# First attention group normalised and rotated at the start instead of behind the gates; the sums of squares of every head taken in two spaced halves

## The chip, the core and the metric

The kernel runs on one core of a Trainium2 chip. The metric is the device time of one execution in microseconds (us). The core's engines work side by side, each through its own queue in order: TensorE (PE in the rows; PEld is its weight load), VectorE (DVE), ScalarE (ACT), GpSimd (POOL), and SyncE (SP), which here issues most of the transfers. POOL issues the rest.

## The reference

Two encoder layers over 512 tokens plus 16 learned meta tokens (T = 528 columns), width 2048, float32. The change lies in layer 0:

```python
def attention_mixer(h, w_in, q_norm, k_norm, w_out, ang_row, ang_col):
    proj = h @ w_in
    q, k, v, gate = jnp.split(proj, [...], axis=-1)      # 16 heads, 8 kv heads, width 128
    q = apply_axial_rope(rmsnorm(q, q_norm), ang_row, ang_col)
    k = apply_axial_rope(rmsnorm(k, k_norm), ang_row, ang_col)
...
    return (o * jax.nn.silu(gate)) @ w_out               # o: softmax attention
```

`h` is the RMS-normalised input. Each key/value head serves two query heads, so there are eight groups of one K, two Q and one V projection. Layer 1 (gated linear attention) is the same in both kernels.

## The kernel before

**Numbers.** Every product is made of three fast matmuls: operands are split in a high and a low part, and hi·hi, hi·lo, lo·hi are summed in PSUM. The normalised, transposed input lies in `uh`/`ul` for the whole layer. A weight block of 8 k-steps is loaded raw into `wraw` (two buffers), cast by ACT to `whi` and subtracted by DVE to `wlo` (three buffers each).

**Order.** A `Clock` decides the order in which the program is written: loops on PE call `clk.step`, generators driven by it (`combine`, `attention`) and calls put off with `clk.after(us, f)` are written in between when their time has come by that clock. `clk.flush` writes all that is still put off. A list scheduler then makes each engine's queue from it, with weights at a higher priority.

**Stages of layer 0.**

1. *Start, 0 to 57 us.* x is transposed and split while the first three column tiles of 128 are accumulated in six PSUM banks. In the kernel before these are gate tiles 0 to 2 (columns 4096 and on); they go to DRAM (`g_d`).
2. *Four projections, 57 to 106 us.* `to_dram` computes K, both Q and V of group 0 and stores them raw (`qkv_d`). Beside it `combine` builds `th`/`tl` on DVE and ACT in eight k-steps: sums of quarters of `uh`/`ul`. Its scratch tiles `x` are four quarter buffers, used in turn (step 2 and step 6 use the same one, `x02`).
3. *Five pairs of gate tiles, 106 to 208 us.* `seven` computes a pair with seven products of 24 matmuls instead of eight. A pair needs four raw quarter blocks, a11, a21, a22 and a12. For the first pair they are loaded into the two `wraw` buffers and into quarter buffers that `combine` has left: a22 in `x00`, a12 in `x02`. The order of products is a11·u, then T2, T3, T4, T1 (from `th`), then a12·u and one more.
4. *Group 0, about 208 to 310 us*, attention of group 0, with the projections for group 1 beside it. `first_group` first loads K and Q back, squares and scales them, and rotates three heads.
5. *Groups 1 to 7, 310 to 795 us*, each attention with the projections for the next group beside it, then output projection and layer 1.

**One head.** `take` makes `qw` (scaled) and `sq` (squares) from PSUM. `rope` swaps neighbouring blocks of 32 partitions with four transfers (`qs<-qw`, issued by SP), multiplies `qw` by cos and `qs` by sin on POOL, and some 6.5 us of the `Clock` later calls `late`: for each half of the columns two matmuls with ones sum the squares over partitions (`ssq`, L310 and L311) and a DVE instruction takes the sums out (L312); then rsqrt on ACT, `qw + qs` (L314), times the rsqrt, split. In the attention stages the `ssq` tile lies in `ps_o`, a pool of one bank which also holds the attention's output `o`, so the second half waits until DVE has read the first, and a following `o` until it has read the second.

Of the kernel before, what the change touches and what calls it, by code (L numbers as in the profile page):

```python
# [35 lines left out]
SLOTS = (3.1, 3.8, 3.8, 3.8, 3.8, 3.8, 3.8, 2.6)  # L36
# [46 lines left out]
def hybrid_encoder(  # L83
# [22 lines left out]
    qkv_d = scratch.tile([4, P, T], F32, name="qkv_d")  # L106
# [12 lines left out]
    rows = const.tile([P, P], F32, name="rows")  # L119
    rows0 = const.tile([KT, P], F32, name="rows0")  # L120
    G.memset(rows, 0.0)
    cols = const.tile([P, P], F32, name="cols")
    nc.sync.dma_start(out=rows0, in_=pre_norm[0].rearrange("(r p) -> r p", p=P))

# [87 lines left out]
    def seven(src, c, ys, th, tl, free):  # L212
# [53 lines left out]
        w = parts(a12)  # L266
        sums(a11, a12, a11)
        add(y1[:, l], product(w, of_u(1, 0)), y1[:, l])
# [26 lines left out]
    def rope(qw, sq, outs, ps_t, wait=6.5):  # L295
# [22 lines left out]
        clk.after(wait, late)  # L318

    def qk_tiles():  # L320
        kh = wk.tile([P, T], F32R, tag="kh", name="kh")
        kl = wk.tile([P, T], F32R, tag="kl", name="kl")

        qh = wk.tile([P, 2 * T], F32R, tag="qh", name="qh")
        ql = wk.tile([P, 2 * T], F32R, tag="ql", name="ql")
# [3 lines left out]
    Q1 = T + META  # L329

    st = ExitStack()
    sp = pool(st, "start")
    s2 = pool(st, "start2", 2)
    ps_g = pool(st, "ps_g", space=PSUM)
    ps_t = pool(st, "ps_t", 2, space=PSUM)
    xt = sp.tile([P, 4, D], F32, name="xt")
# [1091 lines left out]
```

## Time and profile before

| what | value |
|---|---|
| median of 3 runs | 1829.26 us (1827.41 to 1831.79) |
| the profiled execution, its own time | 1830.27 us |
| its span in the trace | 1828.5 us |
| what lies around the span | 1.8 us |
| PE busy | 1769.3 us, 97% of the span |
| mean granted clock of PE | 0.991 of full speed |

The span is what the rows below are cut from: a time of 106 us is 106 us behind the span's start. PE is the engine that is nearly always at work; a microsecond in which it waits, or in which its clock stands at half, is part of the time.

### The profile page before, as it was taken

How to read it: one execution, taken by the hardware profiler on the slowest of the kernel's cores; microseconds unless marked ns; L12 is line 12 of the kernel's file. 1: busy time of each engine (PE TensorE's matmuls, PEld its weight loads, DVE VectorE, ACT ScalarE, POOL GpSimd, SP SyncE). 2: the span in 40 equal slices, each digit the busy share in tenths (PEclk: the TensorE clock that was granted, in tenths of full speed). 3: DMA queues.
4: the chain of work that ended last, by engine and by line, in shares of the span. 5: the costliest groups of instructions: out<-in, count | busy, mean ns of one | idle time of the engine just before them, and what ended most of it. 6: DMA issues, size and time to landing. Idle time of an engine off the chain costs nothing. (4 is left out here: it accounts for less than half of the span.)

```text
span 1828.5 us, 31687 instructions
## 1 busy us (share of the span) xinstructions
PE 1769.3 (97%) x12591; PEld 1662.5 (91%) x12591; DVE 1121.6 (61%) x1904; ACT 950.8 (52%) x1909; POOL 219.7 (12%) x290
## 2 busy tenths in 40 slices
PE   8999899999989999999999999999999999999998
PEld 7999889998989999999999989998898988888886
DVE  4777586665656665752228697768585775764224
ACT  5543465555545554553237634458575775763221
POOL 3100222112121101021111101110010100000000
PEclk9999999999999999999999999999999999999999
DMA  8444433232322223253335344443332332344333
GB/s 254 140 139 118 145 91 97 71 93 77 89 76 81 72 84 99 68 173 93 92 105 169 119 133 128 125 119 97 86 110 77 104 100 77 103 156 165 100 93 127
DMA packets 266660, 203.11 MB, mean 111 GB/s; under 512 B 9900, under 2 KB 239984, under 8 KB 265984
## 3 DMA queue, kind: packets, MB, share of 16 engines
q1 hardware_dynamic: 254768, 162.79, 31.0%
q0 software_dynamic: 11744, 38.30, 6.0%
q8 instruction: 99, 1.62, 0.4%
q14 instruction: 49, 0.40, 0.1%
HBM read 165.47 MB, written 29.09 MB: 106 GB/s over the span
## 5 line engine op out<-in xcount | busy, mean ns | idle before, releaser
L158 PE MATMUL pp<-uh,whi 128*128 128x264 f32 (+1 forms) x2320 | 714.7, 308 | 1.7 <-DVE gr L617 1.6
L159 PE MATMUL pp<-ul,whi 128*128 128x264 f32 (+1 forms) x2320 | 705.1, 304 | 2.2 <-DVE ul L419 2.2
L160 PE MATMUL pp<-uh,wlo 128*128 128x264 f32 (+1 forms) x2320 | 705.8, 304 | 0.4 <-POOL wlo L358 0.3
L136 DVE TENSOR_TENSOR wlo<-wraw,whi 128x1024 fp32r<-128x1024 f32 (+1 forms) x239 | 291.1, 1219 | 312.2 <-ACT whi L135 311.4
L158 PEld LDWEIGHTS pp<-uh,whi 128*128 128x128 f32 x2320 | 440.0, 190 | 18.2 <-DVE gr L617 1.8
L160 PEld LDWEIGHTS pp<-uh,wlo 128*128 128x128 f32 x2320 | 439.9, 190 | 17.5 <-POOL wlo L358 0.6
L159 PEld LDWEIGHTS pp<-ul,whi 128*128 128x128 f32 x2320 | 440.3, 190 | 16.3 <-DVE ul L419 2.8
L135 ACT CAST whi<-wraw 128x1024 fp32r<-128x1024 f32 (+1 forms) x239 | 248.9, 1043 | 319.3 <-PE pp L159 127.7
L135 ACT CAST whi<-x 128x1024 fp32r<-128x1024 f32 x48 | 50.1, 1046 | 70.8 <-PE pp L236 50.1
L631 ACT ACTIVATE pn<-s,mx 128x528 f32<-128x528 f32 (+1 forms) x72 | 50.4, 700 | 57.1 <-DVE mx L628 56.5
L1340 PE MATMUL f<-whi,ul 128*128 128x512 f32 x192 | 75.6, 394 | 0.0
L1338 PE MATMUL f<-whi,uh 128*128 128x512 f32 x192 | 75.5, 393 | 0.0
L1339 PE MATMUL f<-wlo,uh 128*128 128x512 f32 x192 | 75.3, 392 | 0.0
L237 PE MATMUL pp<-uh,wlo 128*128 128x264 f32 x264 | 75.2, 285 | 0.0
L235 PE MATMUL pp<-uh,whi 128*128 128x264 f32 x264 | 75.0, 284 | 0.0
L236 PE MATMUL pp<-ul,whi 128*128 128x264 f32 x264 | 74.7, 283 | 0.0
L136 DVE TENSOR_TENSOR wlo<-x,whi 128x1024 fp32r<-128x1024 f32 x48 | 58.6, 1222 | 20.5 <-ACT whi L135 20.5
L304 POOL TENSOR_TENSOR qw<-qw,cos 128x528 f32<-128x528 f32 x24 | 32.1, 1339 | 293.2 <-DMA qs<-qw 293.2
L628 DVE TENSOR_REDUCE mx<-s 128x1 f32<-128x528 f32 (+1 forms) x72 | 50.7, 704 | 22.3 <-PE s L625 21.3
L645 ACT CAST ph<-pT 128x512 fp32r<-128x512 f32 (+1 forms) x80 | 40.7, 509 | 43.6 <-PE pT L641 34.9
L646 DVE TENSOR_TENSOR pl<-pT,ph 128x512 fp32r<-128x512 f32 (+1 forms) x80 | 47.4, 593 | 21.4 <-ACT ph L645 20.7
L235 PE MATMUL pp<-th,whi 128*128 128x264 f32 x192 | 56.1, 292 | 0.3 <-ACT th L135 0.3
(400 smaller groups left out, 3717.7 us busy)
## 6 DMA issues: line engine op xcount, KB each, us to landing
wraw<-in_attn_w_in_dram SPq DMA_DIRECT2D x82, 512.0 KB, 4.1
wraw<-in_gla_w_in_dram SPq DMA_DIRECT2D x81, 512.0 KB, 3.9
wraw<-in_attn_w_out_dram SPq DMA_DIRECT2D x32, 512.0 KB, 3.8
wraw<-in_gla_w_out_dram SPq DMA_DIRECT2D x32, 512.0 KB, 3.8
x<-in_gla_w_in_dram SPq DMA_DIRECT2D x15, 512.0 KB, 4.3
qs<-qw SPq DMA_DIRECT2D x96, 66.0 KB, 2.6
x<-in_attn_w_in_dram SPq DMA_DIRECT2D x12, 512.0 KB, 4.1
x<-h_d SPq DMA_DIRECT2D x32, 132.0 KB, 3.5
```

The source lines that it names most:

```text
L135: A.copy(hi, src)
L136: V.tensor_tensor(lo, src, hi.bitcast(F32), op=ALU.subtract)
L158: PE.matmul(ps, wh, uh[:, k, a:b], start=first, stop=False)
L159: PE.matmul(ps, wh, ul[:, k, a:b], start=False, stop=False)
L160: PE.matmul(ps, wl, uh[:, k, a:b], start=False, stop=last)
L235: PE.matmul(ps, w[0][:, k], bh[:, k], start=k == 0, stop=False)
L236: PE.matmul(ps, w[0][:, k], bl[:, k], start=False, stop=False)
L237: PE.matmul(ps, w[1][:, k], bh[:, k], start=False, stop=k == KH - 1)
L628: V.reduce_max(mx, s, axis=AX.XY, negate=True)
L1338: PE.matmul(ps, uh[:, k, ts], wh[:, kk], start=(k == 0), stop=False)
L1339: PE.matmul(ps, uh[:, k, ts], wl[:, kk], start=False, stop=False)
L1340: PE.matmul(ps, ul[:, k, ts], wh[:, kk], start=False, stop=(k == KT - 1))
```

## The change

The start accumulates K and both Q of group 0 (columns 2048, 0 and 128) in place of gates 0 to 2. They are evacuated with scale and square (two ACT instructions for each bank in place of one copy) and rotated there, one head after the other with a `clk.flush` after each, with `cos` and `sin` loaded into the start's own pool and the `ssq` tiles in the start's PSUM pool. The rotated tiles stay in a pool of the whole layer (`c0`) through the pairs. `to_dram` then computes gates 0 to 2 and V of group 0. `first_group` is gone, and the transfers of K and Q to DRAM and back with it.

The first pair is told `late=True`: its second product is a12·u, which needs no sums, and T2 comes third; a12·u is copied by ACT and added on DVE.

In `rope` the first half of the sum of squares is put off by 4.4 and the second half, with all that follows, by 6.5 (before: both by 6.5, or 4.5 in `first_group`). `SLOTS[0]`, the spacing of group 0's attention, goes from 3.1 to 3.8; the leads in front of groups 0 and 1 go; V of group 0 is put off by 8.0 in place of 5.0. Tiles of q and k alternate between two pools of one buffer.

```diff
-SLOTS = (3.1, 3.8, 3.8, 3.8, 3.8, 3.8, 3.8, 2.6)
+SLOTS = (3.8, 3.8, 3.8, 3.8, 3.8, 3.8, 3.8, 2.6)
...
-    def seven(src, c, ys, th, tl, free):
+    def seven(src, c, ys, th, tl, free, late=False):
...
         A.copy(y1[:, l], product(w, of_u(0, 0)))
+        if late:
+            w = parts(a12)
+            A.copy(y2[:, l], product(w, of_u(1, 0)))
         add(y1[:, r], product(parts(a11), of_t(T2)), y1[:, l])
+        if late:
+            add(y1[:, l], y1[:, l], y2[:, l])
...
-        w = parts(a12)
+        if not late:
+            w = parts(a12)
         sums(a11, a12, a11)
-        add(y1[:, l], product(w, of_u(1, 0)), y1[:, l])
+        if not late:
+            add(y1[:, l], product(w, of_u(1, 0)), y1[:, l])
...
-        qw = wk.tile([P, T], F32, tag="qw", name="qw", bufs=3)
-        sq = wk.tile([P, T], F32, tag="sq", name="sq", bufs=2)
+        qw = wk.tile([P, T], F32, tag="qw", name="qw", bufs=2)
+        sq = wk.tile([P, T], F32, tag="sq", name="sq", bufs=1 if wk is ws else 2)
...
+        def sums(a, b):
+            ps = ps_q.tile([P, 512], F32, tag=tag, name="ssq")[:, :b - a]
+            PE.matmul(ps, ones_r, sh[:, a:b], start=True, stop=False)
+            PE.matmul(ps, ones_r, sl[:, a:b], start=False, stop=True)
+            V.scalar_tensor_tensor(f[:, a:b], ps, 1.0 / P, erow[:, a:b], op0=ALU.mult, op1=ALU.add)
+
         def late():
-            for a, b in HALVES:
-                ps = ps_o.tile([P, 512], F32, tag="o", name="ssq")[:, :b - a]
-                PE.matmul(ps, ones_r, sh[:, a:b], start=True, stop=False)
-                PE.matmul(ps, ones_r, sl[:, a:b], start=False, stop=True)
-                V.scalar_tensor_tensor(f[:, a:b], ps, 1.0 / P, erow[:, a:b], op0=ALU.mult, op1=ALU.add)
+            sums(*HALVES[1])
             rsqrt_inplace(f)
...
-        clk.after(wait, late)
+        clk.after(4.4, lambda: sums(*HALVES[0]))
+        clk.after(6.5, late)
...
-    group([(w_in0, 4096, P), (w_in0, 4096 + P, 256)], accs, start, 0, halves=3,
+    group([(w_in0, 2048, P), (w_in0, 0, 256)], accs, start, 0, halves=3,
...
+    cos, sin = [ws.tile([P, T], F32, name=n, bufs=1) for n in ("cos0", "sin0")]
+    nc.sync.dma_start(out=cos, in_=rope_cos)
+    nc.sync.dma_start(out=sin, in_=rope_sin)
+    for i in range(3):
+        rope(*(taken(i) if i else head0), qks[0][1][i], ps_t, "t")
+        clk.flush()
     st.close()
...
-    for i, c in enumerate((2048, 0, P, 3072)):
-        to_dram(qkv_d, i, c)
+    for i, (dst, c) in enumerate([(g_d[i], 4096 + i * P) for i in range(3)] + [(v0_d, 3072)]):
+        to_dram(dst, i, c)
...
-        free = seven(w_in0, 4096 + h * P, ys, th, tl, free)
+        free = seven(w_in0, 4096 + h * P, ys, th, tl, free, h == 3)
...
-        lead = first_group(first_outs) if g == 0 else iter([7.0] if g == 1 else [])
-        att = clk.drive(chain(lead, att))
+        att = clk.drive(att)
```

**DVE behind the start.** In the kernel before, `combine` (L204, its first sum) follows right behind `erow`, the last piece of the row norms:

```order
L485 TENSOR_SCALAR erow<-rrow 128x528
L204 TENSOR_TENSOR x_751<-uh,ul 128x1056
L204 TENSOR_TENSOR x_752<-uh,ul 128x1056
L206 TENSOR_TENSOR x_751<-x_751 128x528
L206 TENSOR_TENSOR x_752<-x_752 128x528
```

In the changed kernel the three rotations stand between. These are the last twelve rows up to `combine` (L198 there); L313 takes a sum of squares, L318 is `qw + qs`, L319 the product with the rsqrt, `ql` the low part of a rotated head:

```order
L318 TENSOR_TENSOR qw<-qw,qs 128x528
L319 TENSOR_TENSOR qw<-qw,sq 128x528
L130 TENSOR_TENSOR ql_98<-qw,qh_97 128x528
L130 TENSOR_TENSOR sl<-sq,sh 128x528
L313 SCALAR_TENSOR_TENSOR sq<-ssq,erow 128x264 x2
L130 TENSOR_TENSOR wlo<-wraw,whi 128x1024
L318 TENSOR_TENSOR qw<-qw,qs 128x528
L319 TENSOR_TENSOR qw<-qw,sq 128x528
L130 TENSOR_TENSOR wlo<-wraw,whi 128x1024
L130 TENSOR_TENSOR ql_98<-qw,qh_97 128x512
L130 TENSOR_TENSOR ql_98<-qw,qh_97 128x16
L198 TENSOR_TENSOR x_843<-uh,ul 128x1056
```

What moved: the first instruction of `combine` stands behind the whole of the second and the third head. Six `wlo` stood inside `combine` up to the end of its step 6 in the kernel before; now four of them stand ahead of it, two inside, and two sums of the first pair (L224) inside too.

**SP, from the swaps to the first pair's blocks, in the changed kernel.** L301 is a swap, L147 a raw weight block of a projection, L211 a block of a pair (`x_843` is a22, `x_845` is a12; the bracket names the queues and engines that it waits for):

```order
L301 DMA qs<-qw 32x528 [waits DMAHW1_49,DMAHW2_49,DMAHW0_49,DMAHW7_49,DVE_49,Activation_49]
L301 DMA qs<-qw 32x528
L301 DMA qs<-qw 32x528 [waits DMAHW5_49]
L147 DMA wraw<-in_attn_w_in_dram 128x8x128 [waits DMAHW6_49,DVE_49]
L301 DMA qs<-qw 32x528
L147 DMA wraw<-in_attn_w_in_dram 128x8x128 [waits DVE_49]
L301 DMA qs<-qw 32x528 [waits DMAHW4_49,DMAHW5_49,DMAHW3_49,DMAHW7_49,DVE_49,Activation_49]
L301 DMA qs<-qw 32x528 x3
L147 DMA wraw<-in_attn_w_in_dram 128x8x128 [waits DMAHW6_49,DVE_49]
L211 DMA wraw<-in_attn_w_in_dram 128x8x128 [waits DMAHW0_49,DVE_49]
L211 DMA wraw<-in_attn_w_in_dram 128x8x128 [waits DMAHW5_49,DVE_49]
L211 DMA x_843<-in_attn_w_in_dram 128x8x128 [waits DMASW4_49,DMASW2_49,DMASW6_49,DMASW1_49,DMASW7_49,DMASW0_49,DVE_49]
```

The next row is `x_845`, the load of a12. What moved: the swaps of group 0 stood at the beginning of the attention; here a head's swaps wait for DVE's reading of the head before (one buffer `qs`), one of them stands behind a raw block, and a12, needed sixth before, is needed second.

**PE in the first pair of the changed kernel**, from the end of the first product over six matmuls of scores (`s`) to the second product, which is the first row with a wait:

```order
L232 MATMUL pp<-uh,wlo 128x264
L626 MATMUL s<-kh_95,qh_97 128x264
L627 MATMUL s<-kh_95,ql_98 128x264
L628 MATMUL s<-kl_96,qh_97 128x264
L626 MATMUL s<-kh_95,qh_97 128x264
L627 MATMUL s<-kh_95,ql_98 128x264
L628 MATMUL s<-kl_96,qh_97 128x264
L230 MATMUL pp<-uh,whi 128x264 [waits Activation_49]
L231 MATMUL pp<-ul,whi 128x264
L230 MATMUL pp<-t0h,whi 128x264 [waits Activation_49]
L231 MATMUL pp<-t0l,whi 128x264
L232 MATMUL pp<-uh,wlo 128x264 [waits DVE_49]
```

In the kernel before T2 (`t0h`) came second. Here two of its matmuls come third and fourth within a12·u.

**PE at the third head of a group** (the projections for group 3, beside group 2's attention). Before, eight rows stand between the halves (before the first row here), and five between the second half and the first `o`:

```order
L310 MATMUL ssq<-sh,ones_r 128x264 [waits DVE_49]
L311 MATMUL ssq<-sl,ones_r 128x264
L160 MATMUL pp<-uh,wlo 128x264
L158 MATMUL pp<-uh,whi 128x264
L159 MATMUL pp<-ul,whi 128x264
L160 MATMUL pp<-uh,wlo 128x264
L158 MATMUL pp<-uh,whi 128x264
L661 MATMUL o<-ph,vh 128x272 [waits DVE_49,Activation_49]
```

In the changed kernel 21 rows stand between the halves (before the first row here), and nine between the second half and `o`:

```order
L311 MATMUL ssq<-sh,ones_r 128x264 [waits DVE_49]
L312 MATMUL ssq<-sl,ones_r 128x264
L152 MATMUL pp<-uh,whi 128x264
L153 MATMUL pp<-ul,whi 128x264
L154 MATMUL pp<-uh,wlo 128x264
L152 MATMUL pp<-uh,whi 128x264
L153 MATMUL pp<-ul,whi 128x264
L154 MATMUL pp<-uh,wlo 128x264
L152 MATMUL pp<-uh,whi 128x264
L153 MATMUL pp<-ul,whi 128x264
L154 MATMUL pp<-uh,wlo 128x264
L664 MATMUL o<-ph,vh 128x272 [waits DVE_49,Activation_49]
```

What moved: the second half now waits for a DVE instruction that has had more time, and `o` still follows closely on it. On DVE at this head the order is now first half out, `gr` times `rrow` (L604, a stored gate), `qw + qs`, second half out; before it was `gr`, `qw + qs`, and then both halves out.

## Rows read from the trace of the kernel before

**Rows 1.** Windows: stretch, length, busy PE PEld DVE ACT POOL, PE's clock, DMA:

```profile
57.00:106.00 49.00, 49.00 (x406) 49.00 (x405) 45.17 (x65) 23.00 (x36) 3.50 (x7) 1.00 0.47 144
106.00:208.00 102.00, 102.00 (x841) 102.00 (x840) 74.96 (x87) 38.35 (x41) 9.03 (x18) 1.00 0.42 124
208.00:310.00 102.00, 89.75 (x690) 86.53 (x690) 69.49 (x129) 60.48 (x129) 27.80 (x25) 0.95 0.36 106
310.00:387.00 77.00, 73.32 (x587) 71.94 (x586) 50.47 (x105) 42.87 (x98) 12.70 (x12) 0.98 0.29 83
690.00:795.00 105.00, 100.28 (x811) 97.65 (x810) 70.40 (x142) 57.64 (x130) 10.84 (x10) 1.00 0.32 99
```

**Rows 2.** Waits of PE, 208 to 310 us: total, count, longest:

```profile
PE vps L552 <- DMA vt<-qkv_d: 4.5, 1, 4.5
PE ssq L311 <- DVE sl L136: 3.4, 2, 3.1
```

**Rows 3.** Waits of PE, 310 to 795 us, the longest sum:

```profile
PE ssq L310 <- DVE sq L312: 20.5, 12, 3.4
```

**Rows 4.** Timeline of PE at second halves: start, length, wait in brackets:

```profile
320.37 0.39 PE L310 MATMUL ssq<-sh,ones_r 128*128 128x264 f32 x1 [1.07 <-DVE sq L312]
...
357.93 0.39 PE L310 MATMUL ssq<-sh,ones_r 128*128 128x264 f32 x1 [1.92 <-DVE sq L312]
...
435.14 0.39 PE L310 MATMUL ssq<-sh,ones_r 128*128 128x264 f32 x1 [2.35 <-DVE sq L312]
...
658.60 0.39 PE L310 MATMUL ssq<-sh,ones_r 128*128 128x264 f32 x1 [1.74 <-DVE sq L312]
```

**Rows 5.** Timeline of DVE at the third head whose half PE awaits until 435.14:

```profile
433.13 0.87 DVE L601 TENSOR_TENSOR gr<-gr,rrow 128x528 f32<-128x528 f32 x1 [3.28 <-DMA gr<-g_d]
433.93 0.69 DVE L314 TENSOR_TENSOR qw<-qw,qs 128x528 f32<-128x528 f32 x1
434.66 0.43 DVE L312 SCALAR_TENSOR_TENSOR sq<-ssq,erow 128x264 f32<-128x264 f32 x1
435.69 0.43 DVE L312 SCALAR_TENSOR_TENSOR sq<-ssq,erow 128x264 f32<-128x264 f32 x1 [0.60 <-PE ssq L311]
```

**Rows 6.** Timeline of DVE, 57 to 106 us:

```profile
59.00 2.36 DVE L136 TENSOR_TENSOR wlo<-wraw,whi 128x1024 fp32r<-128x1024 f32 x2
...
62.49 2.42 DVE L204 TENSOR_TENSOR x<-uh,ul 128x1056 f32<-128x1056 f32 x2
...
97.31 1.26 DVE L136 TENSOR_TENSOR t0l<-x,t0h 128x1056 fp32r<-128x1056 f32 x1
```

**Rows 7.** Swaps and rotation: SP's queue in group 0, then the tile `qs`:

```profile
240.10 2.42 SPq L299 DMA_DIRECT2D qs<-qw  x4
...
L305 POOL TENSOR_TENSOR qs<-qs,sin x24: 1297/1316/1853, 223.7 to 725.0; 128x528 f32<-128x528 f32 x24
...
DMA to landing us min/median/max: 1.9/2.6/4.9
```

**Rows 8.** Groups of DVE instructions, 62.4 to 98.6 us: busy, mean ns, idle before:

```profile
L136 DVE TENSOR_TENSOR wlo<-wraw,whi 128x1024 fp32r<-128x1024 f32 x6 | 7.4, 1225 | 1.8 <-ACT whi L135 1.8
```

**Rows 9.** The page: cast of a quarter block (busy, mean ns), its transfer (us to landing):

```profile
L135 ACT CAST whi<-x 128x1024 fp32r<-128x1024 f32 x48 | 50.1, 1046 | 70.8 <-PE pp L236 50.1
...
x<-in_attn_w_in_dram SPq DMA_DIRECT2D x12, 512.0 KB, 4.1
```

**Rows 10.** Timeline of PE, first matmuls of the first pair's two first products:

```profile
106.11 0.28 PE L235 MATMUL pp<-uh,whi 128*128 128x264 f32 x1
...
109.01 0.29 PE L235 MATMUL pp<-t0h,whi 128*128 128x264 f32 x1
```

**Rows 11.** Windows of PE alone around its longest wait in group 0:

```profile
222.00:225.00 3.00, 3.00 (x15) 0.50 0.00 0
```

**Rows 12.** Timeline of DVE in group 0, the subtraction `sl` of two heads:

```profile
215.94 0.71 DVE L136 TENSOR_TENSOR sl<-sq,sh 128x528 fp32r<-128x528 f32 x1
...
236.50 1.80 DVE L136 TENSOR_TENSOR sl<-sq,sh 128x528 fp32r<-128x528 f32 x1
```

More of the change, by code (lines that the diff above doesn't have):

```diff
@@ L1 @@
 import heapq
-from itertools import chain
 from contextlib import ExitStack
@@ L293, in take, with rope @@
         return qw, sq, evac
-    def rope(qw, sq, outs, ps_t, wait=6.5):
+    def rope(qw, sq, outs, ps_q, tag):
         qs = wk.tile([P, T], F32, tag="qs", name="qs", bufs=1)
@@ L317, in late, with qk_tiles @@
                 split(hi, lo, qw[:, a:b])
-        clk.after(wait, late)
[L320 to L325, printed above, removed]
+        clk.after(4.4, lambda: sums(*HALVES[0]))
+        clk.after(6.5, late)
+    def qk_tiles(p, n):
+        kh, kl = [p.tile([P, T], F32R, name=f"k{w}{n}") for w in "hl"]
+        qh, ql = [p.tile([P, 2 * T], F32R, name=f"q{w}{n}") for w in "hl"]
         outs = ([(kh, kl, 0, T)], [(qh[:, :T], ql[:, :T], 0, T)],
@@ L335, in hybrid_encoder @@
     ps_t = pool(st, "ps_t", 2, space=PSUM)
+    rows = sp.tile([P, P], F32, name="rows")
+    rows0 = sp.tile([KT, P], F32, name="rows0")
+    G.memset(rows, 0.0)
+    nc.sync.dma_start(out=rows0, in_=pre_norm[0].rearrange("(r p) -> r p", p=P))
     xt = sp.tile([P, 4, D], F32, name="xt")
@@ L347, in load_w @@
     def load_w(i, k, m, queue=nc.sync):
-        raw, c, n = ((raw0, 4096, P), (raw1, 4096 + P, 256))[i]
+        raw, c, n = ((raw0, 2048, P), (raw1, 0, 256))[i]
         queue.dma_start(out=raw[:, k * n:(k + m) * n].rearrange("p (k n) -> p k n", n=n),
@@ L466, in hybrid_encoder, with taken @@
     V.tensor_scalar(col(QN), col(QN), SCALE, None, op0=ALU.mult)
-    for i in range(3):
-        y = s2.tile([P, T], F32, tag="y", name="y", bufs=3)
+    def taken(i):
+        qw, sq, evac = take(col(QN if i else KN))
         for j, ps, a, b in banks:
             if j == i:
-                A.copy(y[:, a:b], ps)
-        nc.gpsimd.dma_start(out=g_d[i], in_=y)
+                evac(ps, a, b)
+        return qw, sq
+    head0 = taken(0)
     V.reduce_sum(ss, ssq, axis=AX.X)
@@ L492, in hybrid_encoder @@
     th, tl = [ta.tile([P, KH, 4 * HALF], F32R, name=f"t0{w}") for w in "hl"]
+    quarters = [ta.tile([P, 4 * HALF], F32, name=f"x0{i}") for i in range(4)]
     yp = pool(la, "yp0", 2)
-    quarters = [ta.tile([P, 4 * HALF], F32, name=f"x0{i}") for i in range(4)]
     def y_tiles():
@@ L544, in values @@
         if g == 0:
-            nc.sync.dma_start(out=vt, in_=qkv_d[3])
+            with tc.high_priority(AHEAD):
+                nc.sync.dma_start(out=vt, in_=v0_d)
         else:
@@ L564, in late @@
                                    op0=ALU.mult, op1=ALU.subtract)
-        clk.after(1.2 if g else 5.0, late)
+        clk.after(1.2 if g else 8.0, late)
         return vh, vl, vm
     def qkv(g):
-        qk, outs = qk_tiles()
-        vv = values(g) if g == 1 else None
+        qk, outs = qks[g % 2]
         for i, c in enumerate((2048 + g * P, 2 * g * P, (2 * g + 1) * P)):
@@ L573, in qkv @@
             project(w_in0, c, HALVES, evac)
-            rope(qw, sq, outs[i], ps_t)
-        return qk, vv or values(g)
-    def first_group(outs):
-        qws = []
-        for i in range(3):
-            qws.append(wk.tile([P, T], F32, tag="qw", name="qw", bufs=3))
-            nc.gpsimd.dma_start(out=qws[i], in_=qkv_d[i])
-        for i in range(3):
-            yield 4.6 if i else 1.0
-            one_head(qws[i], outs[i], i)
-        yield 5.0
-    def one_head(qw, outs, i):
-        sq = wk.tile([P, T], F32, tag="sq", name="sq", bufs=2)
-        A.activation(sq, qw, AF.Square)
-        A.activation(qw, qw, AF.Copy, scale=col(QN if i else KN))
-        rope(qw, sq, outs, ps_t, 4.5)
+            rope(qw, sq, outs[i], ps_o, "o")
+        return qk, values(g)
     def stored_gates(hs, held):
```

17 lines of the change are left out of this document (8 added, 9 removed).

## The prediction

> **What bounds the kernel now.** I read the windows by stage first [rows 1]. From 57 to 208 us PE is busy in all of it and its clock is full: 49.00 of 49.00 and 102.00 of 102.00 us. DVE is close behind at the beginning (45.17 of 49.00). From 208 to 310 us, where group 0's heads are loaded back and rotated, PE is busy 89.75 of 102.00 us and its clock stands at 0.95: 12.25 us idle and 0.05 x 102 = 5.1 us of clock are 17.4 us lost. The stages behind lose less: 3.68 + 0.02 x 77 = 5.2 us of 77 (310 to 387), and 4.72 of 105 (690 to 795), which for 102 us is 6.9 and 4.6.
>
> Then I read what PE waits for. In group 0 the longest waits belong to what the change moves: 4.5 us for V loaded back, 3.4 for the parts of a sum of squares [rows 2]. In groups 1 to 7 one reason holds 20.5 us in 12 waits [rows 3]: the second half of a sum of squares needs the one bank that DVE has not read. The timeline of these waits has two kinds [rows 4]. Seven are at first or second heads (320.37, 1.07 us, is the first); five are at third heads (from 357.93, 1.92 us, to 658.60, 1.74 us; 11.2 us by adding all five, which leaves 20.5 - 11.2 = 9.3 to the seven). At the third heads DVE is held by something else: the instruction that would free the bank (434.66) stands behind a gate that waited 3.28 us for its transfer, and behind `qw + qs` [rows 5].
>
> **What the start will cost.** `combine` now begins at 62.49 [rows 6]. In the changed kernel its first instruction stands behind the third head's rotation, so I follow that chain. Head 0's swaps stand in SP's queue behind raw blocks whose buffers come free with the subtractions of 59.00 to 61.36 [rows 6], so they start at about 61.4. Four issues take 2.42 us, landing 2.6, two multiplications on POOL 1.32 each [rows 7], `qw + qs` 0.69 [rows 5]: 8.4 us, and head 0's sum is there at 69.8. Head 1's swaps wait for DVE's reading of head 0, and its last one stands behind a raw block that waits for a subtraction queued behind head 0; I add 1.5 us for that (`qw` times rsqrt, about 0.7, and most of a subtraction of 1.2): 69.8 + 9.9 = 79.7. Head 2 has no such block: 88.1. Behind it come the product with the rsqrt, a weight subtraction and the last of the split, 0.7 + 1.2 + about 0.8: `combine` begins at **90.8**. Landing at its shortest, 1.9, in all three heads gives 88.7, at its longest, 4.9, 97.7 [rows 7].
>
> From its beginning to the end of step 6, which reads `x02` last, `combine` took 62.49 to 97.31 + 1.26 = 98.57, 36.1 us [rows 6]. In that lay six weight subtractions, 7.4 us, and 1.8 us idle [rows 8]. Now two of the six and two sums of blocks lie in it, 4 x 1.22 = 4.9: 36.1 - 7.4 - 1.8 + 4.9 = 31.8. So `x02` comes free at 90.8 + 31.8 = 122.6. Only then can a12 be loaded, 4.1 us, and cast; PE's queue has two matmuls of T2 early in this product, which want a second cast, 1.05 each [rows 9]: 122.6 + 4.1 + 2.1 = 128.8. PE will have ended the first product at about 112: 106.11 + 2.90 [rows 10], 1.5 for twelve matmuls of sums of squares that come here from group 0 (24 in a product of 2.90, so 0.12 each), and some 2 us of small waits for those sums. PE then stands some 16 us. Two products less four matmuls are 5.3, so the third ends at 134.1; in the kernel before it ended at 106.11 + 3 x 2.90 = 114.8. Shift: **19.3**. After such a wait PE does not run at once: after 4.5 us its clock stood at 0.50 for three us [rows 11], which is 1.5 us lost, for the edges of that stretch I take 1.7. **Loss 21.0**; with the bounds of the swaps 18.9 to 27.9. Waits of PE before the stall cost nothing by themselves as long as the stall covers them.
>
> The rest of the start I cost at nothing. Evacuation takes six more ACT instructions, and ACT is busy 23.00 of 49.00 us there [rows 1]; as the first projection fills banks of its own, PE does not ask for them, and without that cover it would be some 2 us, inside the stall. POOL, 3.50 of 49.00 busy [rows 1], has room for six multiplications. Two loads of tables and the saved trips of K and Q through DRAM are on queues that PE does not wait for here. `late=True` leaves the products at seven; its copy and its addition lie beside products.
>
> One rule speaks against the place of the rotations. The trace first: beside a multiplication on POOL, DVE's subtraction `sl` took 1.80 us, otherwise 0.71 [rows 12]. The Trainium skill, "SBUF — State Buffer", section "Who interferes with whom", says that a DVE instruction with two SBUF inputs contends with a GpSimd instruction that reads SBUF, and that the loser is blocked for the whole instruction. By it every one of six multiplications that meets a DVE instruction would push the chain. By that rule, the trace agrees with 1.80 against 0.71. At 1.1 us each that is up to 6.6 us more; it is a rival below. I put it at nothing in the sum because DVE in this chain is mostly waiting for POOL.
>
> **What comes back.** (1) Group 0's stage loses 17.4 now. Without load, square and rotation it should be like its neighbours, 4.6 to 6.9 [rows 1]. A gain of 10.5 to 12.8; I take 12. V's transfer is given priority and its use is put off; SLOTS, the leads and the pools of q and k belong to this term. (2) The twelve matmuls, 1.5. (3) At the seven first and second heads the halves stand some 21 to 27 matmuls apart instead of 6 to 14. At 0.12 us that is 2.6 us and more, where these waits were 1 to 1.7: **9.3** gone. Were DVE as late there as at third heads, none of it would go. (4) At third heads the second half will run, but the next user of the bank, `o`, follows after nine matmuls, and it needs the second half read by DVE, still behind the gate and `qw + qs`. Before, DVE had two halves to read after those, with a matmul pair between: 434.66 to 436.12. Now one, to about 435.1 [rows 5]. So 1.0 us of each of the five goes at best, the rest turns into a wait of `o`. I take 0.7: **3.5**, with bounds of 0 and 11.2. With two `qw` buffers for three, a head's evacuation may wait for the head one before; three projection banks cover it.
>
> Sum of gains: 12 + 1.5 + 9.3 + 3.5 = **26.3**. Net: 21.0 - 26.3 = -5.3. The profiled execution took 1830.27, so 1825.0; the median of the runs lies 1.0 below it: **1824** us.
>
> **Rivals.**
>
> *More comes back.* The spacing frees the third heads wholly (11.2 for 3.5), or landing is short. For: after the first half is read early DVE has one thing less. Against: the gate's transfer is as late as it was. -5.3 - 7.7 gives 1816; with the short chain too, 1814.
>
> *The waits only move.* Group 0's attention keeps half of what it lost, since its softmax chain, not the rotations, sets it (other waits than those in [rows 2] hold the rest of 12.25), and third heads give nothing: gains 6 + 1.5 + 9.3 = 16.8, net +4.2, 1833.5 and slower. With only one of the two it is 1828 to 1830, the same.
>
> *The chain of swaps is longer.* This is the mechanism for the other side: swaps behind raw blocks, each head behind the one before, and everything of the first pair behind them. With landings near 4.9 `combine` begins at 97.7, the loss is 27.9 and the time 1831. It decides from a beginning of about 99.5, where the loss is 30 and the kernel is slower by over 3.7 us; later than 92.4 it is already no longer faster. For: SP issues the four in turn, and raw blocks of 512 KB land beside them. Against: 2.6 is the median of 96 in a kernel with the same neighbours.
>
> *POOL and DVE block each other* in the start, by the rule above: 3.3 to 6.6 us more, 1828 to 1831, the same.
>
> *The early a12 does not do what it says.* Its product was to need no sums, yet its block must wait for `combine`. If the block lands early all the same, T2 still waits for the last step of `combine`, which ends at least a sum and a subtraction behind step 6, 1.22 + 1.26 [rows 6, 8]: only some 3 to 4 us better, 1820. This is part of the first rival's chance.
>
> **How the numbers follow.** About 0.2%, 3.7 us, can be told from no change here. My forecast 1824, its own range 1820 to 1828, has a chance of 0.43 (0.28 faster, 0.15 the same); more comes back 0.20 (faster); waits only move 0.16 (half the same, half slower); a longer chain 0.15 (0.05 the same, 0.10 slower); POOL and DVE 0.06 (the same). Faster 0.48, the same 0.34, slower 0.18. The range reaches from the first rival's bound, 1814, to a little over the second's, 1834.
>
> **What the profile will show.** `combine`'s first sum at 88 to 93 us; the wait of PE for the cast of a12 between 112 and 129, 13 to 18 us in one piece; the third product's end near 136. In the stage of group 0, PE idle near 5 us and no rotation. In groups 1 to 7 almost no wait of second halves, and a new one of `o` for the sum of squares, 5 to 9 us in about five pieces. I am wrong if the stall is under 10 or over 20 us, if group 0's stage still idles over 9 us, or if the new wait of `o` sums to as much as the old one, 20 us.

## The result, and the profile after

The changed kernel takes 1831.83 us (median of 14 runs, 1829.46 to 1833.52), the kernel before 1827.7 in the 14 runs beside it (1822.85 to 1834.05): a ratio of 1.0022 [1.0011, 1.0032]. It is slower by 4.1 us, a little more than the 0.2% (3.7 us) that the prediction takes as the least that can be told. The time lies in the range; the direction was forecast the other way.

The profiled execution after took 1830.58 us, that of before 1830.27. They differ by 0.3 us where the medians differ by 4.1, because the one of before lies 2.6 above its median and the one of after 1.3 below. The traces therefore show how the two times come about, not the 4.1 us themselves.

The windows after (columns as in [rows 1]):

```profile
57.00:106.00 49.00, 45.25 (x368) 44.65 (x367) 34.68 (x56) 25.19 (x48) 9.79 (x10) 1.00 0.39 113
106.00:208.00 102.00, 88.07 (x709) 87.55 (x708) 81.78 (x98) 37.41 (x41) 4.33 (x8) 0.93 0.38 114
208.00:310.00 102.00, 95.51 (x766) 94.41 (x766) 64.88 (x116) 52.62 (x106) 19.90 (x25) 0.97 0.36 107
310.00:387.00 77.00, 73.45 (x594) 72.76 (x594) 48.49 (x100) 42.82 (x98) 14.61 (x14) 0.98 0.32 91
690.00:795.00 105.00, 101.01 (x822) 98.95 (x821) 71.17 (x144) 57.99 (x130) 12.28 (x13) 1.00 0.32 98
```

The first two stages, full before, now lose: 3.75 us of idle PE, then 13.93 and a clock of 0.93. The third lost 12.25 and now loses 6.49.

What PE waits for, over the whole run:

```profile
PE o L664 <- DVE sq L313: 20.5, 7, 4.3
PE pp L230 <- ACT whi L129: 13.8, 1, 13.8
PE ssq L311 <- ACT sh L129: 3.0, 2, 1.7
```

The wait of the second halves [rows 3] is gone. In its place stands one for the same DVE instruction and of the same sum, 20.5 us, but at `o`, seven times, once for each group whose heads are rotated in the attention. Six of the seven, 16.2 us, lie behind 310 us, where the 20.5 us of [rows 3] lay.

I followed the time lost by how much later than before the n-th matmul of PE begins. Both kernels have 12,591, so the rows pair off. A pair is not always the same work: by the 1000th the changed kernel has done the twelve matmuls of group 0's sums of squares and six of its scores, and 18 fewer of the projections and products. The shift in us (minus is earlier):

| n-th matmul | 1000 | 1600 | 2000 | 2200 | 2400 | 3200 | 4000 | 4800 | 6200 | 12400 |
|---|---|---|---|---|---|---|---|---|---|---|
| changed | 20.6 | 20.5 | 7.9 | 13.8 | 10.4 | 8.1 | 4.4 | 1.1 | 0.1 | 0.3 |

The start costs 20.5. By the end of group 0's stage (2400) 10.1 has come back, over groups 1 to 7 another 10.3, behind them nothing. Within group 0's stage 12.6 were back by the 2000th matmul; 5.9 of them were lost again by the 2200th, where the first of the seven waits at `o` lies.

The waits do not make up all of the 10.3 us of groups 1 to 7. Between the 2400th and the 6200th matmul PE's waits fall from 25.9 to 20.4 us, and those of second halves and of `o` alone from 19.4 to 16.2. The other 4.8 us lie in PE's rows without their waits (474.5 against 469.7 us for the same 3,800 matmuls), with a mean granted clock of 0.98 from 310 to 795 us in both kernels.

**The start.** DVE's timeline:

```profile
70.55 0.71 DVE L318 TENSOR_TENSOR qw<-qw,qs 128x528 f32<-128x528 f32 x1 [6.62 <-POOL qs L307]
...
80.83 0.71 DVE L318 TENSOR_TENSOR qw<-qw,qs 128x528 f32<-128x528 f32 x1 [3.71 <-POOL qs L307]
...
87.05 2.26 DVE L130 TENSOR_TENSOR wlo<-wraw,whi 128x1024 fp32r<-128x1024 f32 x1 [0.67 <-ACT whi L129]
89.23 0.70 DVE L318 TENSOR_TENSOR qw<-qw,qs 128x528 f32<-128x528 f32 x1
...
92.49 2.42 DVE L198 TENSOR_TENSOR x<-uh,ul 128x1056 f32<-128x1056 f32 x2
...
123.16 1.25 DVE L130 TENSOR_TENSOR t0l<-x,t0h 128x1056 fp32r<-128x1056 f32 x1
```

`qw + qs` needs a head's swaps and POOL's multiplication of them; DVE stands idle ahead of the first two. `combine` begins at 92.49 and its step 6 ends at 124.41. PE's timeline shows the price in one row, the first matmul of the second product, behind 13.79 us of waiting for the cast of a12:

```profile
129.75 0.59 PE L230 MATMUL pp<-uh,whi 128*128 128x264 f32 x1 [13.79 <-ACT whi L129]
```

**A third head.** DVE at the head of [rows 5] (group 3's third, beside group 2's attention):

```profile
438.66 0.43 DVE L313 SCALAR_TENSOR_TENSOR sq<-ssq,erow 128x264 f32<-128x264 f32 x1
442.09 0.83 DVE L604 TENSOR_TENSOR gr<-gr,rrow 128x528 f32<-128x528 f32 x1 [3.00 <-DMA gr<-g_d]
442.84 0.69 DVE L318 TENSOR_TENSOR qw<-qw,qs 128x528 f32<-128x528 f32 x1
443.46 0.42 DVE L313 SCALAR_TENSOR_TENSOR sq<-ssq,erow 128x264 f32<-128x264 f32 x1
```

PE and POOL beside it, one row of each engine's timeline:

```profile
444.03 0.39 PE L664 MATMUL o<-ph,vh 128*128 128x272 f32 x1 [2.75 <-DVE sq L313]
```

```profile
441.07 1.28 POOL L307 TENSOR_TENSOR qs<-qs,sin 128x528 f32<-128x528 f32 x1
```

The first half is read early, at 438.66, as meant. The second is read at 443.46, behind a gate that waited 3.00 us for its load and behind `qw + qs`, whose input POOL finished only at 442.35. So two late things stand ahead of that reading, and `o` waits for it.

It is not the same two at every third head. At the last three waits (2.29, 2.49 and 1.34 us) no gate stands there; `qw + qs` alone waits, 3.00 to 4.15 us, for POOL:

```profile
588.63 0.71 DVE L318 TENSOR_TENSOR qw<-qw,qs 128x528 f32<-128x528 f32 x1 [3.02 <-POOL qs L307]
```

### The profile page after: what moved, and what is told of

The parts are those of the page before. It is cut to its first block, busy times and chain, and to the rows that moved or that the text cites. A ratio compares the mean times of both kernels' runs of the same rounds, so it can differ in the third digit from the quotient of the medians.

```text
span 1828.7 us, 31700 instructions
## 1 busy us (share of the span) xinstructions
PE 1764.1 (96%) x12591; PEld 1661.6 (91%) x12591; DVE 1118.0 (61%) x1904; ACT 951.1 (52%) x1910; POOL 214.6 (12%) x284
## 5 line engine op out<-in xcount | busy, mean ns | idle before, releaser
L152 PEld LDWEIGHTS pp<-uh,whi 128*128 128x128 f32 x2320 | 439.1, 189 | 19.8 <-DVE gr L620 1.6
L230 PE MATMUL pp<-uh,whi 128*128 128x264 f32 x264 | 75.8, 287 | 13.8 <-ACT whi L129 13.8
L230 PEld LDWEIGHTS pp<-uh,whi 128*128 128x128 f32 x264 | 50.3, 191 | 14.0 <-ACT whi L129 14.0
L649 DVE TENSOR_TENSOR pl<-pT,ph 128x512 fp32r<-128x512 f32 (+1 forms) x80 | 47.5, 594 | 22.7 <-ACT ph L648 22.3
```

Of the source, the lines that this page charges most:

```text
L152: PE.matmul(ps, wh, uh[:, k, a:b], start=first, stop=False)
L230: PE.matmul(ps, w[0][:, k], bh[:, k], start=k == 0, stop=False)
```

## The experiments

The first table has the medians of what the runs came to, start against placing of the sums (before, 1827.25 to 1828.34 in the groups of runs, is 1827.7 here):

| | halves together | halves spaced | halves and rest in three parts |
|---|---|---|---|
| old start | 1827.7 | 1816.4 | 1802.7 |
| new start | 1841.8 | 1831.8 | 1810.9 |

### Which part costs, which part gives

**unspaced**: the new start alone; both halves at 6.5 again.

```diff
+            sums(*HALVES[0])
             sums(*HALVES[1])
-        clk.after(4.4, lambda: sums(*HALVES[0]))
```

> The changed kernel with both halves of every sum of squares put off by 6.5 again, the new start kept. My theory from the two traces: the spacing gave back about 10 us in groups 1 to 7 (the shift of the n-th matmul fell from 10.4 to 0.1 us there), so without it the kernel is about 14 us slower than the kernel before (some 1842 us, ratio 1.0077), and the waits of the second half for DVE are back at about 20 us. Rival: the spacing only renamed the waits (20.5 us in total before and after); then this run equals the changed kernel, 4 us slower than before, and its waits add up to the same PE time.

1841.81 us, 1.0085 [1.0072, 1.0097] to before. The start loses 20.4 at the 1000th matmul; 6.3 of it comes back by the 2400th, and over groups 1 to 7 nothing. The second halves are waited for once more:

```profile
PE ssq L311 <- DVE sq L313: 25.2, 14, 3.4
```

**old_start_spaced**: the spacing alone, in the kernel before.

```diff
+        clk.after(wait - 2.1, lambda: sums(*HALVES[0]))
         clk.after(wait, late)
```

> The kernel before with nothing but the halves spaced (first half 2.1 of the clock earlier than the rest: 4.4 and 6.5, in first_group 2.4 and 4.5). Theory: spacing is worth 10 us wherever the start lies (the new start without it took 1841.8, with it 1831.8), so some 1817 us, ratio 0.9945; what the new start costs by itself is then 14 us. Rival: the spacing needs the new start (in the old one group 0's heads share the bank with the halves, and new waits of o eat the gain): no faster than 1824.

1816.39, 0.9936 [0.9919, 0.9952]. The two parts are opposite in sign: the start costs 14.1, the spacing gives 11.3 alone and 10.0 on top of the start. Here too PE's wait moves to `o` (16.7 us in six waits), so the spacing is worth more than the waits by themselves, as in the changed kernel.

**split**: the changed kernel with the second half's sum and reading in a step of its own, ahead of the gate and of `qw + qs` on DVE.

```diff
-        clk.after(4.4, lambda: sums(*HALVES[0]))
-        clk.after(6.5, late)
+        clk.after(3.4, lambda: sums(*HALVES[0]))
+        clk.after(5.4, lambda: sums(*HALVES[1]))
+        clk.after(7.5, late)
```

> The changed kernel with the work of a head put off in three parts: first half of the sum 3.4, second half 5.4, the rest (rsqrt, qw + qs, product, split) 7.5. On DVE the second half's reading then stands ahead of the gate times rrow and of qw + qs at the third heads, and 23 matmuls ahead of o. Theory: the seven waits of o (20.5 us in the changed kernel) come from that order on DVE alone, so they go, with about 1 us of half clock behind each: 20 to 27 us faster than the changed kernel, some 1805 to 1812 us. Rival: o waits for something else at the same time (its own operands, or the gate's transfer through another path); then less than 10 us are gained and a wait of another name stands there.

1810.9, 0.9911 [0.9898, 0.9925], 20.9 below the changed kernel. DVE at the same head:

```profile
430.09 0.43 DVE L313 SCALAR_TENSOR_TENSOR sq<-ssq,erow 128x264 f32<-128x264 f32 x1
433.36 0.71 DVE L604 TENSOR_TENSOR gr<-gr,rrow 128x528 f32<-128x528 f32 x1 [2.84 <-DMA gr<-g_d]
433.99 0.70 DVE L317 TENSOR_TENSOR qw<-qw,qs 128x528 f32<-128x528 f32 x1
```

The gate waits as long as before (2.84), but the reading now stands ahead of it, and PE's waits over 205 to 800 us are

```profile
PE vps L573 <- ACT vt L568: 7.8, 5, 1.9
PE o L664 <- DVE sq L313: 2.0, 1, 2.0
```

So 18.5 of 20.5 us at `o` are gone, and a new wait of 7.8 at V's transposes takes some of it back. The granted clock gives something too. These are the windows of PE alone, the changed kernel first:

```profile
205.00:800.00 595.00, 567.64 (x4586) 0.98 0.31 92
205.00:800.00 595.00, 581.67 (x4784) 1.00 0.34 98
```

0.02 of 595 us is some 12 us at full speed. The edit moves both halves about a microsecond of the `Clock` earlier and the rest one later, so the order on DVE is not all that it changes; pool_add and both_moved below leave these times as they are and gain 13.8 and 15.3.

**old_start_split**: the same three parts in the kernel before (first half at `wait - 3.1`, second at `wait - 1.1`, rest at `wait + 1.0`).

> The kernel before with the work of a head put off in three parts (first half 3.4, second half 5.4, the rest 7.5; in first_group 1.4, 3.4 and 5.5). Theory: the three parts brought 21 us against two under the new start, some 4 to 5 of them in group 0's stage that the old start spends otherwise; so 15 to 20 below the old start with two parts, 1797 to 1803 us. The new start would then be 8 to 14 us the slower with three parts too. Rival: with the old start the same order on DVE does not come about, and it stays above 1810.

1802.72, 0.986 [0.9841, 0.9879]: the shortest of all with old_start_best below (1802.78), and it needs nothing of the new start, which costs 8.2 us with three parts.

### What the start's chain is made of

**noswap**: the 12 swaps of the start are left out (POOL multiplies `qw` by `sin` instead).

> The changed kernel, leaving out the twelve swaps of partitions in the start group (its heads are multiplied without the exchange, so group 0's q and k are not the reference's); everything else is as it was. Theory: the stall before the first pair's second product (13.8 us) is set by the chain swap, landing, POOL, DVE of three heads ahead of combine. Without about 5 us per head combine begins at 77 to 80 us instead of 92.5, the stall falls to 0 to 3 us, and the kernel is 12 to 15 us faster than the changed one, 1817 to 1820. Rival: DVE's and ACT's own work for the three heads sets it; then combine begins at 87 or later and less than 6 us are gained.

1827.94, 1.0005 [0.9996, 1.0013], only 3.9 below the changed kernel. My theory, that `combine` would begin at 77 to 80 because the swaps' landing fills DVE's idle time, fell: it began at 85.94.

```profile
85.94 1.25 DVE L198 TENSOR_TENSOR x<-uh,ul 128x1056 f32<-128x1056 f32 x1
```

Without a swap DVE was still idle for 9.4 us of 62.5 to 85.9, by hand-offs with POOL, ACT and PE in turn. And of the 6.5 us by which `combine` began earlier only 2.8 were left at the end of its step 6 (121.62), for the reason that bufs shows next.

**bufs**: `qw`, `sq` and `qs` of the start with three buffers each, so that the heads need not follow one another.

```diff
+        qw = wk.tile([P, T], F32, tag="qw", name="qw", bufs=3 if wk is ws else 2)
+        sq = wk.tile([P, T], F32, tag="sq", name="sq", bufs=3 if wk is ws else 2)
+        qs = wk.tile([P, T], F32, tag="qs", name="qs", bufs=3 if wk is ws else 1)
```

> The changed kernel with three buffers each for qw, sq and qs in the start, so that the three heads' swaps need not wait for one another; work and order of heads are otherwise the same. Theory after the run without swaps: the time ahead of combine is three heads in a row, each waiting for its own transfers, POOL and ACT while DVE idles (13.7 us idle between 62 and 92.5 in the changed kernel). Overlapped, combine begins at 78 to 83 us, the wait for a12 falls from 13.8 to 2 to 6, and the kernel gains 7 to 11 us on the changed one: 1821 to 1825. Rival: DVE has to do the same work before step 6 of combine, and weights and rotations just change places: less than 4 us gained.

1828.65, 1.0002 [0.999, 1.0013]: 3.2 gained. DVE's idle time ahead of `combine` fell from 14.0 us to 5.2, but `combine` began only 7.6 us earlier (84.86): DVE's own instructions became longer where POOL multiplies beside them. DVE, then POOL:

```profile
71.40 1.81 DVE L318 TENSOR_TENSOR qw<-qw,qs 128x528 f32<-128x528 f32 x1 [1.21 <-POOL qs L307]
...
75.24 2.01 DVE L130 TENSOR_TENSOR wlo<-wraw,whi 128x1024 fp32r<-128x1024 f32 x1
77.17 1.83 DVE L130 TENSOR_TENSOR kl<-qw,kh 128x528 fp32r<-128x528 f32 x1
78.92 0.69 DVE L318 TENSOR_TENSOR qw<-qw,qs 128x528 f32<-128x528 f32 x1
```

```profile
72.61 1.80 POOL L307 TENSOR_TENSOR qs<-qs,sin 128x528 f32<-128x528 f32 x1
...
76.13 2.31 POOL L307 TENSOR_TENSOR qs<-qs,sin 128x528 f32<-128x528 f32 x1
```

Of the 7.6 us only 3.7 reach the end of step 6, which now lies at 120.70 (124.41 in the changed kernel):

```profile
119.45 1.25 DVE L130 TENSOR_TENSOR t0l<-x,t0h 128x1056 fp32r<-128x1056 f32 x1
```

Four weight subtractions and three sums of blocks, 1.22 us each, lie in `combine` up to there, where the changed kernel has two and two. They had stood ahead of it or behind. So the rival of this run came about as well: weights and rotations changed places on a DVE that has little room.

**norot**: rotation and normalisation of the start's three heads left out; they are split as they come.

> The changed kernel leaving out the rotation and the normalisation of the start's three heads (they are scaled and split only, so group 0's attention is not the reference's): no swaps, no sums, no multiplications, about 6 us of DVE work and 13 us of its waiting gone. Theory: the stall of the first pair is DVE's time ahead of combine's step 6, so combine begins at 65 to 67 and runs as in the kernel before, the wait for a12 falls from 13.8 to under 2 us, and the time is 15 to 20 us below the changed kernel, 1812 to 1817. Rival: the stall comes from the first pair itself (a12's block in the quarter buffer of step 6): a wait of 5 us or more stays.

1809.54, 0.9904 [0.9881, 0.9928], 22.3 below the changed kernel. `combine` begins at 66.81, and the wait of 13.8 us is gone:

```profile
66.81 2.42 DVE L198 TENSOR_TENSOR x<-uh,ul 128x1056 f32<-128x1056 f32 x2
```

At the 1000th matmul it is 2.8 us behind the kernel before, where the changed kernel is 20.6 behind. So 17.9 us of the start's loss come from the rotation and normalisation of these heads; which of the two is not separated. Leaving out the swaps, more buffers, and the old order of products (late_off) each give 3 to 4 us.

**late_off**: `late=False`; a12·u keeps its place of before, sixth.

> The changed kernel with the first pair in the old order of products (late=False): T2 second, a12 sixth. Theory: T2 needs the last step of combine, which ended at 128.75 us in the changed kernel; a12's cast ended at about 129.7. So the two orders wait for nearly the same: within 2 us of the changed kernel. Rival A: the early a12 covers some of the wait, and without it the kernel is 3 us (one product) slower. Rival B: the early a12's block, which has to wait for combine's step 6, is what delays; then this run is 3 us or more faster.

1827.99, 1.0006 [0.9996, 1.0015], 3.8 below the changed kernel: PE waits 10.8 us instead of 13.8. Bringing a12·u forward delays the first pair: its block goes into `x02`, which `combine` reads until its step 6, and its cast ended at 129.70; T2, second in late_off, could begin at 127.43.

**all**: `bufs`, the three parts, and the first pair's blocks in other quarter buffers, a12 in the one that comes free first.

```diff
-    free += [q[:, :1024] for q in quarters]
+    free += [quarters[i][:, :1024] for i in (1, 2, 0, 3)]
```

> The new start with three buffers, a12 loaded into the quarter buffer that combine leaves after step 4 (a22 after step 5), and the head's work in three parts. Theory: 1811 with three parts alone; the second product then follows the first without a stall, T2 waits until about 119 in place of the third product's end at 135, so some 12 us less: 1797 to 1801, level with the old start with three parts. Rival: the start stays DVE-bound and only 5 us come back, 1806.

1807.34, 0.9878 [0.9858, 0.9897]. PE's stall fell to 4.5 us in two waits, yet the old start with the same three parts is 4.6 us shorter: the new start is not made free by this.

### What the second half's reading waits for

**pool_add**: `qw + qs` on POOL outside the start.

```diff
-            V.tensor_tensor(qw, qw, qs, op=ALU.add)
+            (V if wk is ws else G).tensor_tensor(qw, qw, qs, op=ALU.add)
```

> The changed kernel with qw + qs done by POOL behind its two multiplications in place of DVE, in all heads but the start's. Theory: by the same two obstacles, the gate's transfer still holds DVE; the second half is then read 0.6 us earlier (one addition less ahead of it): 3 to 6 us faster than the changed kernel, 1826 to 1829. Rival: qw + qs alone is what delays; then most of the 20 us are gained.

1818.08, 0.9946 [0.9931, 0.9961], 13.8 below the changed kernel, where I had thought 3 to 6. The waits at `o` fell to half:

```profile
PE o L664 <- DVE sq L313: 9.7, 4, 2.5
```

The three waits with no gate ahead of them are gone. The four that are left stand where a gate waited 2.85 to 2.92 us for its load; DVE at the third head of group 3 reads the half right behind it:

```profile
439.86 1.07 DVE L604 TENSOR_TENSOR gr<-gr,rrow 128x528 f32<-128x528 f32 x1 [2.85 <-DMA gr<-g_d]
440.85 0.42 DVE L313 SCALAR_TENSOR_TENSOR sq<-ssq,erow 128x264 f32<-128x264 f32 x1
```

I had counted only the 0.7 us that `qw + qs` takes. Where POOL's multiplication ends behind the gate, or where there is no gate, DVE's wait for POOL goes too.

**gate_sp**, **gate_early** and **gr3** try the other late thing, the gate's load: asked for through SP instead of POOL; both of a group's loads asked for at once; three `gr` buffers for two. **both_moved**, **gate_early_pool_add** and **gr3_pool_add** are the same three on top of pool_add.

```diff
-            nc.gpsimd.dma_start(out=gr, in_=g_d[h])
+            nc.sync.dma_start(out=gr, in_=g_d[h])
```

```diff
-            gr = wa.tile([P, T], F32, tag="gr", name="gr", bufs=2)
+            gr = wa.tile([P, T], F32, tag="gr", name="gr", bufs=3)
```

> The changed kernel with the stored gates (gr) loaded through SP's queue in place of POOL's, where each load stood behind a multiplication of the gate before. Theory: at a third head two things stand ahead of the second half on DVE, the gate (its transfer landed at 442.1 at the head that PE awaited until 444.0) and qw + qs (POOL was done at 442.35). They end at nearly the same time, so taking away the transfer's lateness alone gains at most 0.5 us a head: within 5 us of the changed kernel, 1827 to 1832. Rival: the gate alone is late; then most of the 20 us are gained.

> Both of these changes together, the halves still spaced by 4.4 and 6.5. Theory: only with both gone does DVE read the second half at once, the seven waits of o fall from 20.5 to under 5 us, and the kernel is 16 to 24 us faster than the changed one, 1808 to 1816, like the run in three parts. Rival: the three parts helped by their other positions, not by the order on DVE; then this run gains under 10 us.

> The changed kernel with both stored gates of a group asked for at once, so that a gate's load no longer stands on POOL behind the multiplication of the gate before it (the load through SP had come 0.7 us earlier only: it stood behind others there). Theory: at third heads the second half still stands behind qw + qs, which POOL lets go at about 442.35 of the changed kernel's trace, so this alone gains 0 to 5 us: 1827 to 1832, and the waits of o stay above 15 us. Rival: the gate is the last obstacle; then 15 us or more are gained.

> The same together with qw + qs done by POOL (alone: 1818.1 us, o still waiting 9.7 us in four waits at heads where the gate was late). Theory: the four remaining waits of 2.2 to 2.5 us go, with some half clock behind each: 7 to 11 us faster than with qw + qs on POOL alone, 1807 to 1811, level with the run in three parts (1810.9), which had the same order by another way. Rival: the four waits are not the gate's; then it stays at 1815 to 1819.

> The changed kernel with three buffers for the gates (gr). In the runs with the earlier request the load still came right behind the multiplication that frees its buffer (437.56 behind 435.94), so it was the buffer that made it late; with a third one a gate is loaded one gate earlier. Theory: qw + qs still stands ahead of the second half, so only 0 to 5 us are gained: 1827 to 1832.

> Three buffers for the gates and qw + qs on POOL. Theory: the four waits of o that were left with qw + qs on POOL (9.7 us, each behind a gate that waited for its transfer) go, with some half clock: 7 to 11 us faster than 1818, so 1807 to 1811. Rival: those waits are not the gate's; 1815 to 1819 again.

| | alone | on top of pool_add |
|---|---|---|
| load through SP | 1828.12, 1.0006 [0.9997, 1.0016] | 1816.54, 0.9938 [0.9923, 0.9953] |
| both loads at once | 1832.02, 1.0025 [1.0013, 1.0037] | 1817.89, 0.995 [0.9933, 0.9967] |
| three buffers | 1831.54, 1.0017 [1.0005, 1.003] | 1817.84, 0.9944 [0.9928, 0.996] |

None made the gate early, so none tells its share. Through SP its product began 0.7 us earlier at the third head (441.39), but `qw + qs` still stood behind it and the second half was read at 443.39, against 443.46. What gives gate_sp its 3.7 us, with 20.3 us still waited at `o`, stays open. In gr3_pool_add DVE still waits for the load:

```profile
441.39 0.71 DVE L604 TENSOR_TENSOR gr<-gr,rrow 128x528 f32<-128x528 f32 x1 [2.95 <-DMA gr<-g_d]
```

With a third buffer the load is still issued at 438.19, behind POOL's multiplication of the gate before it. What the gate alone holds is argued from the rows (the four waits, 9.7 us, that pool_add leaves behind a late gate) and not shown by a run.

**old_start_tuned** (old_start_split with `rope`'s wait 6.0 for 4.5 in group 0, and V's 2.6 for 1.2) and **old_start_best** (old_start_split with pool_add and gate_early) tried to go below 1802.72.

> The old start with a head's work in three parts, and two more numbers: first_group's heads put off by 6.0 in place of 4.5 (halves 2.9 and 4.9), and V's transposition by 2.6 in place of 1.2 after its projection. In the trace of the old start in three parts PE still waits 3.8 us for the first sum of squares of group 0 and 7.2 us in four waits for V's copy. Theory: these go, with some half clock behind them: 1790 to 1798 us. Rival: they come back as other waits of the attention, since everything behind them moves too: 1800 to 1806.

> The old start with a head's work in three parts (1802.7 us), qw + qs on POOL and both gates of a group asked for at once. Theory: in three parts DVE's order is already right, so these two add 0 to 4 us: 1799 to 1803. Rival: the later qw + qs of POOL delays the next group's scores: 1805 or more.

1803.24, 0.9864 [0.9847, 0.988], and 1802.78, 0.987 [0.9842, 0.9897]: no gain by either. In old_start_best the reading already stands ahead of both late things, and moving `qw + qs` and the gates' requests gives nothing more; old_start_tuned moved other waits and gave nothing either, where I had thought 5 to 13 us less.

## Why the prediction was wrong

**The loss was right.** `combine` began at 92.49 against 90.8, step 6 ended at 124.4 against 122.6, the second product began at 129.75 against 128.8, PE stood 13.8 us in one piece (13 to 18 forecast), and behind it the clock was 0.50 for three us. PE ended its first product at 116.0 and not at 112, which the stall covered. The prediction counts the 1.5 us of the twelve matmuls of the sums in its loss and again in its gains; by n-th matmuls they fall out of both. So its loss of 21.0 is 19.5 by that table, and 20.5 was measured. norot shows that the rotation and normalisation ahead of `combine` cause 17.9 of it. What I named as the chain's main part was less right: without the swaps the kernel is 3.9 us shorter, with more buffers 3.2; the rest is hand-offs and DVE's own work, which only changes its place.

**The first and second heads were right.** No wait of a second half is left in groups 1 to 7; the 9.3 us there are gone.

**The third heads failed: this is the step that turned the sign.** I took 3.5 us as gained there, since DVE would have one reading fewer behind the gate. The five that lost 11.2 us at the second half now lose 14.9 at `o` (3.12, 2.75, 4.20, 2.29, 2.49), and the last group's adds 1.34: 5.0 more where I had 3.5 less. I compared when DVE would be ready, and not when PE would arrive. DVE does have one reading fewer behind the gate, but PE comes to `o` sooner. At the third head shown, PE's matmuls ahead of the wait begin 8.1 us later than their pairs before, the gate's product 9.0 later (442.09 against 433.13 [rows 5]), and the first `o` is the 3246th matmul instead of the 3250th. That PE is closer because its stop at the first head (1.30 us at 415.93 before) is gone fits the pairing, where PE's shift falls there from 9.7 to 8.1; no run shows it by itself. I had named this wait, at 5 to 9 us in five pieces, and named 20 us as a sign of being wrong; it is 20.5 in seven. split and pool_add confirm what PE waits for: with the reading ahead of the gate and `qw + qs` 2.0 us are left, with `qw + qs` alone out of the way 9.7.

**Group 0's stage was put too high.** I took 12, to be like its neighbours; 10.1 came back by its end. It is the same step that failed: 12.6 were back by the 2000th matmul. But like its neighbours meant with their third head as well. Group 1's heads are rotated beside it, and PE, whose rows of this stretch are

```profile
299.00:302.00 3.00, 2.62 (x11) 0.50 0.00 0
302.00:305.00 3.00, 3.00 (x18) 0.62 0.00 0
```

stood 4.32 us at `o` until 299.38 and then lost about 1.3 (half of 299.38 to 302) + 0.38 x 3 = 2.4 us to the clock. Before, no such wait shows in this stage; that PE's other waits there covered it is my reading and not shown.

Together: 10.1 + 10.3 = 20.4 back for 24.8 forecast (26.3 less the 1.5 of the twelve matmuls). The net of -5.3 became +0.1 by these sums, near the 0.3 that the two profiled executions show. That the miss is no larger is in part luck: by their waits groups 1 to 7 gave 9.3 - 5.0 = 4.3 us for 12.8 forecast, and the rest of their 10.3 are shorter waits elsewhere and shorter rows of PE, for which the prediction had no term. Of the medians' 4.1 the traces tell nothing; that stays open. Of my rivals *the waits only move* (1833.5, slower) came nearest. It had third heads give nothing, and they gave less than that. It had group 0's stage keep half of what it lost, and it kept 6.49 of 12.25 us idle, though 4.32 of these are a third head's wait and not the softmax chain.

**POOL against DVE.** I put this at nothing, because DVE mostly waits for POOL in this chain. In the changed kernel that holds but for one row, the `wlo` of 2.26 us where 1.22 is usual. As soon as bufs lets the heads overlap, five DVE instructions grow by 4.8 us together. DVE's idle time up to the end of step 6 falls by 8.4 us there, and the end comes 3.7 earlier; the growth is the larger part of the difference. The Trainium skill, "SBUF — State Buffer", section "Who interferes with whom", has a DVE instruction with two SBUF inputs contend with a GpSimd instruction that reads SBUF. These rows agree with that, and POOL's instructions were longer as well (1.80 and 2.31 us).

**The early a12** costs 3.8 us (late_off). Its rival named the place, a block that must wait for `combine`, but not a price for that: I counted the early product as no worse than the old order, and it made the wait 3 us longer.

## What to carry to other kernels

When a wait is taken away, ask at the next instruction of the same engine whether its own releaser is any earlier; if the releasing engine is held by something else, the wait only moves on. What frees a PSUM bank should stand, on its in-order engine, ahead of anything that can wait for a transfer or another engine: here taking the second half's reading ahead of these gave 14 us with the old start and 21 with the new. And a piece of work moved to where it seems to have room must be followed to the first instruction queued behind it: three short heads ahead of `combine` put PE 20 us back.

## What the runs showed of the hardware

In bufs a DVE instruction of 0.7 us took 1.5 to 1.8 beside POOL's multiplications, and a subtraction of 1.22 took 2.0; POOL's own, 1.3 us alone, took up to 2.31 there. Both engines lose, and for five DVE instructions of the start this came to 4.8 us.

PE's clock fell to half, 0.50, at five of the seven waits at `o` in the changed kernel, and stayed full at the other two (2.49 and 1.34 us). The length of the wait does not tell them apart: it fell behind one of 2.29 us (until 589.83) and not at one of 2.49 (until 660.76). The windows behind the wait of 2.75 us, of 2.29 and of 2.49:

```profile
444.00:447.00 3.00, 2.97 (x14) 0.54 0.02 5
591.00:594.00 3.00, 3.00 (x16) 0.50 0.00 0
661.00:664.00 3.00, 3.00 (x26) 1.00 0.02 5
```

So the wait of 2.75 us cost about 1.4 us more in the three us behind it (0.46 x 3), and five of the seven waits are dearer than their rows say.
